# Two projections as seven block products, their weight sums, branch merge and residual carried by accumulating transfers

## The chip, the cores and the metric

The kernel runs on one core of one Trainium2 chip. Its engines are TensorE (PE in the profile; PEld is its loading of weights), VectorE (DVE), ScalarE (ACT), GpSimd (POOL) and SyncE (SP, which here only starts transfers). The metric is the device time of one execution in microseconds (us). The kernel before took 1541.7 us as the median of three runs (1539.01 to 1544.57).

## The reference

One layer of an encoder block on 1024 tokens and a model width of 1024. An attention branch and a gated recurrence branch are computed from one input projection; the change lies behind both, where they are projected, merged and projected again:

```python
y_a = einsum('bsc,cd->bsd', o_a * silu(g_a), w_proj_a)           # 512 -> 1024
o_b = rms_norm(o_fwd + o_bwd, hg_norm_w) * silu(g_b)
y_b = einsum('bsc,cd->bsd', o_b, w_proj_b)                       # 1024 -> 1024
merged = sigmoid(zgate_a) * y_a + sigmoid(zgate_b) * y_b
h_res = h_res + einsum('bsd,de->bse', merged, w_out)             # 1024 -> 1024
```

All is float32 at the kernel's edges. Products are computed at float32r speed: each operand is split into a high part (its rounding to float32r) and a low part (the rest), and one product becomes three matmuls: high x high, high x low, low x high.

## The kernel before

**Tiles.** Everything is in tiles of 128 partitions x 512 float32 (256 KB). A weight tile ("page") is loaded from DRAM into `raw`, ScalarE writes its high part `whi`, and GpSimd or VectorE the low part `wlo = raw - whi`; the two rings hold nine pages (`RING`). A matmul is 128 x 128 weights against 128 x 512; a group of them adds up in one PSUM bank.

**Order.** No scheduler runs on the chip. While the program is built, a planner (`Plan`, `Builder`) keeps an estimated clock for each engine. The main line issues matmuls; `tick` lets waiting tasks (`b.task(engine, inputs, function, priority, room)`) issue as soon as their inputs are, by the estimate, nearly ready. The order that comes out is fixed: each engine then works through its own instructions strictly in that order, and an instruction that waits for a semaphore holds up all behind it on its engine. For SP and GpSimd the same holds of starting transfers. SP's transfers take turns on eight semaphores, and each waits for the one eight before it. In the trace nearly all instructions carry line 56, the recording helper, so they are told apart by tile names.

**The end of the kernel.** After the last recurrence head and the last gate pages of the input projection come three projections, one behind the other, 960 matmuls in all:

- y_a: 8 output pages j x 2 token halves, 4 x 3 matmuls each (192). `evac_ya` multiplies the bank with the sigmoid gate (`sgl`, loaded from the scratch tensor `sgD`) into `ma`.
- y_b: the same 16 groups of 8 x 3 matmuls (384). The operands `sh`, `sl` are split from `ld`, loaded from `obD`, the branch's transposed output. `evac_yb` multiplies with the gate on VectorE, adds `ma` on GpSimd, and splits the sum into `mh` and `ml` (ScalarE, VectorE).
- out: 2 column halves e x 8 token tiles t, 8 x 3 matmuls each (384). `evac_out` adds the input tile `xr` on VectorE and SP stores the result.

The norm weight `hwc` is folded into w_proj_b's pages while they are split (`b.scales`). w_proj_b's low parts come from VectorE for that reason, those of w_proj_a and w_out from GpSimd. PSUM is three banks for groups of matmuls (`b.gps`) and five for the rest (`b.bank`).

Of the kernel before, what the change touches and what calls it, by code (L numbers as in the profile page):

```python
# [113 lines left out]
class Plan:  # L114
# [24 lines left out]
    def note(self, key, op, args, kw):  # L139
# [6 lines left out]
        out, ins = aps[0], aps[1:]  # L146
# [5 lines left out]
        n = _free(out)  # L152
        pace, late = 0.2, 0.1
# [57 lines left out]
class Builder:  # L211
# [361 lines left out]
def hybrid_block(ctx, tc, a, out):  # L573
# [78 lines left out]
    consts.tile([128, 48], F32, name="pad")  # L652
    eps = consts.tile([128, 1], F32, name="eps")
# [39 lines left out]
    xs = {}  # L693
# [135 lines left out]
    pos = 0  # L829
# [1013 lines left out]
    for h in range(8):  # L1843
# [6 lines left out]
        for u in range(2):  # L1850
            b.run_unit([T_group(pos, u, evac_q(h, u), u == 1)])
        pos += 2
    OA, OB = {}, {}
    ectx = {}

    def end_start():
        bctx.close()
        ectx["ep"] = ep = ctx.enter_context(tc.tile_pool(name="end", bufs=1))
        ectx["ld"] = b.ring(ep, "ld", 6, [128, 512])
        for k in range(8):  # L1860
            b.task("sp", [oaD], lambda k=k: split_load(OA, k % 4, k // 4, oaD[k % 4, k // 4],
                                                       lambda n: ep.tile([128, 512], F32R, tag="L", name=n, bufs=17)),
                   4, ectx["ld"].soon)

    def split_load(to, j, half, src, new):
        t = ectx["ld"].get()
        s_.dma_start(t, src)
        b.task("act", [t], lambda: split_store(to, j, half, t, new), 4)

    def split_store(to, j, half, t, new):  # L1870
        hi, lo = new(b.name("sh")), new(b.name("sl"))
        a_.activation(hi, t, AF.Copy)
        v_.tensor_tensor(lo, t, hi.bitcast(F32), op=OP.subtract)
        ectx["ld"].done(t)
        to[j, half] = (hi, lo)

    n = 0
    for j in range(TAIL, 8):
        for half in range(2):
            b.run_unit([T_group(pos, half, evac_sg(1, j, half), half == 1)])  # L1880
# [5 lines left out]
        end_start()  # L1886
        b.drain()
    hctx.close()
    assert pos == b.ops - 40, pos

    ep = ectx["ep"]
    ob = ctx.enter_context(tc.tile_pool(name="endo", bufs=1, side="right"))
    MA, MH, ML = {}, {}, {}
    for half in range(2):
        for h in range(8):
            k = 8 * half + h
            b.task("sp", [obD], lambda h=h, half=half: split_load(  # L1900
                OB, h, half, obD[h, half], lambda n: ob.tile([128, 512], F32R, name=n)), 4, ectx["ld"].soon)
    def sig_load(w, j, half):
        t = ep.tile([128, 512], F32, tag="sg", name=b.name("sgl"), bufs=4)
        s_.dma_start(t, sgD[w, j, half])
        b.task("act", [t], lambda: (a_.activation(t, t, AF.Sigmoid), open_.add((w, j, half))), 1)
        return t

    def three(wp, xs, c):
        (wh, wl), (xh, xl) = wp, xs
        return [(wh[:, c:c + 128], xh), (wh[:, c:c + 128], xl), (wl[:, c:c + 128], xh)]  # L1910

    def evac_ya(j, half, sg):
        def f(ps):
            t = ep.tile([128, 512], F32, tag="Hh", name=b.name("ma"), bufs=18)
            b.until(lambda: (0, j, half) in open_)
            v_.tensor_tensor(t, ps, sg, op=OP.mult)
            b.gps.done(ps)
            MA[j, half] = t
        return f

    def evac_yb(j, half, sg):
        def f(ps):
            b.until(lambda: (1, j, half) in open_)
            v_.tensor_tensor(sg, ps, sg, op=OP.mult)
            b.gps.done(ps)
            ma = MA.pop((j, half))
            g_.tensor_tensor(sg, sg, ma, op=OP.add)
            hi = ep.tile([128, 512], F32R, tag="Hh", name=b.name("mh"), bufs=18)
            lo = ep.tile([128, 512], F32R, tag="L", name=b.name("ml"), bufs=17)
            a_.activation(hi, sg, AF.Copy)  # L1930
            v_.tensor_tensor(lo, sg, hi.bitcast(F32), op=OP.subtract)
            MH[j, half], ML[j, half] = hi, lo
        return f

    sgs, open_ = {}, set()
    seq = [(0, j, half) for j in range(8) for half in range(2)] + [(1, j, half) for j in range(8) for half in range(2)]

    def ahead(k):
        while len(sgs) < min(len(seq), k + 3):
            sgs[seq[len(sgs)]] = sig_load(*seq[len(sgs)])  # L1940

    k = 0
    for w in range(2):
        for j in range(8):
            for half in range(2):
                ahead(k)
                sg = sgs[w, j, half]
                k += 1
                if w == 0:
                    gr = dict(k=4, step=lambda d, half=half: three(b.w[pos], OA[d, half], 128 * d),  # L1950
                              evac=evac_ya(j, half, sg), need=lambda d: pos + 1)
                    if half:
                        gr["free"] = lambda d: pos + (d + 1) // 4
                else:
                    gr = dict(k=8, step=lambda d, half=half: three(b.w[pos + d // 4], OB[d, half], 128 * (d % 4)),
                              evac=evac_yb(j, half, sg), need=lambda d: pos + d // 4 + 1,
                              ready=lambda half=half: all((h, half) in OB for h in range(8)))
                    if half:
                        gr["free"] = lambda d: pos + (d + 1) // 4
                b.run_unit([gr])  # L1960
            pos += 1 if w == 0 else 2

    def evac_out(e, t, x):
        def f(ps):
            o = stage.get()
            v_.tensor_tensor(o, ps, x, op=OP.add)
            b.gps.done(ps)
            s_.dma_start(out[128 * t:128 * t + 128, 512 * e:512 * e + 512], o)
            stage.done(o)
        return f  # L1970

    for e in range(2):
        grs = []
        for t in range(8):
            half, c = divmod(t, 4)
            x = ep.tile([128, 512], F32, tag="sg", name=b.name("xr"), bufs=4)
            s_.dma_start(x, a["x"][t, :, 512 * e:512 * e + 512])

            def step(d, half=half, c=c):
                wh, wl = b.w[pos + d]  # L1980
                s = slice(128 * c, 128 * c + 128)
                return [(MH[d, half][:, s], wh), (MH[d, half][:, s], wl), (ML[d, half][:, s], wh)]

            gr = dict(k=8, step=step, evac=evac_out(e, t, x), need=lambda d: pos + d + 1)
            if t >= 6 and (e == 0 or t == 7):
                gr["free"] = lambda d: pos + d + 1
            if t < 6 or e == 1:
                b.run_unit([gr])
            else:
                grs.append(gr)  # L1990
        if grs:
            b.run_unit(grs)
        pos += 8
    b.drain()


# [101 lines left out]
```

## Time and profile before

| quantity | value |
|---|---|
| median of three runs | 1541.7 us |
| profiled execution, span | 1541.9 us |
| PE busy | 1502.3 us (97%), 8109 matmuls |
| DVE busy | 964.9 us (63%) |
| ACT busy | 806.4 us (52%) |
| POOL busy | 433.2 us (28%) |
| DMA | 186.05 MB, mean 121 GB/s |
| last three projections | from 1320.6 us to the end |

The profile gives for each engine its busy time, for groups of equal instructions their number, mean duration and the idle time ahead of them with what ended it, and for transfers the time from issue to landing. Tile names stand without buffer numbers: `gp` is a PSUM bank of a matmul group. Matmuls are pipelined: the duration that is shown for one overlaps the next, so the distance from start to start is what one costs in a row of them.

### The profile page before, as it was taken

To read this page: it belongs to the slowest core of one execution; us is meant where nothing else is said; L and a number is where in the kernel's file an instruction comes from. 1 tells how busy PE (TensorE), PEld (TensorE's weight loads), DVE (VectorE), ACT (ScalarE), POOL (GpSimd) and SP (SyncE) were. 2 spreads that over 40 slices of the span, in tenths; PEclk is the share of its full clock that TensorE was granted. 3 is DMA by queue.
4 is the path that set the end of the run, shared out by engine and by line. 5 is a ranking of instruction groups with operands and counts; after the bars stand their busy time and mean duration, and the time that the engine had idled before them with its cause. 6 is when DMAs were issued, how large, how long until landed. Compare 5 with 4: busy or idle time off the path is not lost. (4 is left out here: it accounts for less than half of the span.)

```text
span 1541.9 us, 22959 instructions
## 1 busy us (share of the span) xinstructions
PE 1502.3 (97%) x8109; PEld 1232.8 (80%) x8109; DVE 964.9 (63%) x1937; ACT 806.4 (52%) x1665; POOL 433.2 (28%) x424
## 2 busy tenths in 40 slices
PE   8999999999999999999989999999989999999999
PEld 7788888777778787888867788878878878888887
DVE  6791778687887834544333558889888886633211
ACT  5542667566676646776722255556554742733210
POOL 0022333232334230110113452444233432013320
PEclk9999999999999999999989999999999999999999
DMA  5443242442424457564256531131311312933232
GB/s 197 132 164 111 97 142 84 135 120 61 135 69 110 109 163 242 191 214 150 83 150 216 173 117 41 42 100 52 96 28 42 109 49 68 328 107 105 84 119 92
DMA packets 163767, 186.05 MB, mean 121 GB/s; under 512 B 42763, under 2 KB 99107, under 8 KB 163652
## 3 DMA queue, kind: packets, MB, share of 16 engines
q1 hardware_dynamic: 156228, 184.13, 38.2%
q10 hardware_dynamic: 7424, 0.45, 0.3%
q8 instruction: 64, 1.05, 0.3%
q14 instruction: 51, 0.42, 0.1%
HBM read 128.60 MB, written 60.66 MB: 123 GB/s over the span
## 5 line engine op out<-in xcount | busy, mean ns | idle before, releaser
L56 POOL TENSOR_TENSOR wlo<-raw,whi 128x512 fp32r<-128x512 f32 x119 | 160.6, 1356 | 431.6 <-ACT whi L56 412.0
L56 POOL TENSOR_TENSOR wlo<-qraw,whi 128x512 fp32r<-128x512 f32 x100 | 139.8, 1406 | 293.0 <-ACT whi L56 263.6
L56 PE MATMUL gp<-whi,hh 128*128 128x512 f32 x344 | 141.2, 411 | 2.8 <-ACT hh L56 1.4
L56 ACT ACTIVATE whi<-raw 128x512 fp32r<-128x512 f32 x136 | 85.0, 625 | 104.7 <-PE gp L56 79.4
L56 PE MATMUL gp<-hh,whi 128*128 128x512 f32 x336 | 137.8, 410 | 0.0
L56 PE MATMUL gp<-whi,hl 128*128 128x512 f32 x344 | 135.9, 395 | 1.3 <-DVE hl L56 1.3
L56 PE MATMUL gp<-wlo,hh 128*128 128x512 f32 x344 | 135.6, 394 | 0.0
L56 PE MATMUL gp<-hh,wlo 128*128 128x512 f32 x336 | 132.0, 393 | 0.0
L56 PE MATMUL gp<-hl,whi 128*128 128x512 f32 x336 | 131.6, 392 | 0.0
L56 ACT ACTIVATE whi<-qraw 128x512 fp32r<-128x512 f32 x140 | 86.0, 624 | 54.0 <-DVE qraw L56 33.6
L56 DVE CUSTOM_DVE_ANT_0 as<-sc,abias 128x192 f32<-128x192 f32 (+2 forms) x192 | 56.2, 348 | 92.8 <-PE sc L56 57.5
L56 ACT ACTIVATE stage<-gp 128x512 f32<-128x512 f32 x60 | 35.4, 594 | 113.6 <-PE gp L56 92.5
L56 ACT ACTIVATE as<-as,neg 128x192 f32<-128x192 f32 (+2 forms) x192 | 83.5, 438 | 7.9 <-DVE neg L56 7.9
L56 DVE TENSOR_TENSOR qraw<-qraw,qraw 128x512 f32<-128x512 f32 x80 | 67.3, 843 | 30.7 <-POOL wlo L56 23.6
L56 PEld LDWEIGHTS gp<-whi,hh 128*128 128x128 f32 x344 | 65.5, 190 | 24.1 <-issue 5.9
L56 PEld LDWEIGHTS gp<-whi,hl 128*128 128x128 f32 x344 | 65.4, 190 | 16.3 <-DVE hl L56 2.2
L56 PEld LDWEIGHTS gp<-wlo,hh 128*128 128x128 f32 x344 | 65.7, 191 | 12.2 <-issue 0.2
L56 PE MATMUL gp<-sh,whi 128*128 128x512 f32 x192 | 74.7, 389 | 0.0
L56 PE MATMUL gp<-sl,whi 128*128 128x512 f32 x192 | 74.7, 389 | 0.0
L56 PE MATMUL gp<-sh,wlo 128*128 128x512 f32 x192 | 74.7, 389 | 0.0
L56 PEld LDWEIGHTS gp<-hh,wlo 128*128 128x128 f32 x336 | 63.4, 189 | 14.0
L56 PEld LDWEIGHTS gp<-hh,whi 128*128 128x128 f32 x336 | 63.7, 190 | 11.4
(257 smaller groups left out, 3980.3 us busy)
## 6 DMA issues: line engine op xcount, KB each, us to landing
raw<-in_w_in_dram SPq DMA_DIRECT2D x112, 256.0 KB, 2.7
qraw<-in_w_in_dram SPq DMA_DIRECT2D x80, 256.0 KB, 4.3
qkD<-ny SPq DMA_DIRECT2D x48, 256.0 KB, 2.1
igD<-stage SPq DMA_DIRECT2D x32, 256.0 KB, 2.0
ig<-igD SPq DMA_DIRECT2D x32, 256.0 KB, 4.4
sgl<-sgD SPq DMA_DIRECT2D x32, 256.0 KB, 3.6
sgD<-stage SPq DMA_DIRECT2D x26, 256.0 KB, 2.0
ak<-qkD SPq DMA_DIRECT2D x6, 1024.0 KB, 7.9
```

Of the source, the lines that this page charges most:

```text
L56: got = f(*args, **kw)
```

## The change

The first projection (y_a) keeps its 192 matmuls, now with all groups of token half 0 first. Each of the two 1024 x 1024 projections is cut into 2 x 2 blocks of 512 and computed by seven block products in place of eight (Winograd's form of Strassen's scheme). A product is 4 groups u of 12 matmuls: 336 matmuls in place of 384 for each projection. `SEVEN` is their order. With weight blocks W11, W12, W21, W22 (first figure: half of the inner dimension) and data blocks X(token half, inner half):

| product | weights | data |
|---|---|---|
| 11 | W11 | X00 |
| 21 | W21 | X01 |
| T2 | W11 + W12 + W22 | X10 - X00 - X11 |
| T1 | W11 + W12 | X10 - X11 |
| T3 | W12 + W22 | X00 - X10 |
| 22 | W22 | X01 + (the T2 data) |
| T4 | W21 + W11 + W12 + W22 | X11 |

- **Weight sums** are made by transfers that add to what lies at their destination (`more`, issued on GpSimd's queue): T3's page is W12 with W22 added from DRAM, T2's is W11 with T3's page added from SBUF, T4's is W21 with T2's page added, T1's is a second copy of W12 with W11 added from DRAM. That is 16 such transfers for each projection, issued in the order T3 and T2 by turns (i = 0 to 3), T4, T1.
- **Data sums** (16 for each projection) are made on VectorE, in place. All 28 pages and 28 data tiles of each projection are split into high and low parts, all low parts now on VectorE; before it was 16 pages and 16 data tiles.
- **Evacuation.** Products that add to a bank that is used again are copied out by ScalarE (11, T2, T1) and combined on VectorE (21, T3, 22); T4 leaves the result in the bank.
- **Branch merge**: 16 accumulating transfers add the gated y_b to `ma`, in place of 16 additions on GpSimd.
- **Residual**: for three of the four output blocks the input is added by accumulating transfers from DRAM (12), for the fourth on VectorE as before.
- The gate ring `sg` has three buffers; `hwc` is applied when the recurrence output is evacuated; PSUM is reopened as four and four banks ahead of y_a; the planner counts an issue on GpSimd as 1.0 us.

In the built program PE has 96 instructions fewer, VectorE 108 more, ScalarE 72 more; GpSimd loses 32 subtractions and additions and issues 60 transfers; SP has four fewer. Up to the first matmul of y_a the order on every engine is the same in both programs, but for the early loads that the new ending needs.

```diff
-            self.t[key] = start + 0.08
+            self.t[key] = start + (1.0 if key == "pool" else 0.08)
...
-    items += [wpa[i] for i in range(8)] + [wpb[i] for i in range(16)] + [wo[i] for i in range(16)]
+    items += [wpa[i] for i in range(8)]
...
-    for i in range(16):
-        b.scales[b.ops - 32 + i] = hwc
...
-        a_.activation(t, ps, AF.Copy)
+        a_.activation(t, ps, AF.Copy, scale=hwc)
...
+        ectx["acc"] = b.ring(ep, "acc", 8, [128, 512])
+        ectx["xh"] = b.ring(ep, "xh", 8, [128, 512], F32R)
+        ectx["xl"] = b.ring(ep, "xl", 8, [128, 512], F32R)
+        ectx["sg"] = b.ring(ep, "sg", 3, [128, 512])
...
+    psum(4)
...
+    rawq = b.ring(ob, "eraw", 18, [128, 512])
...
+    SEVEN = ("11", "21", "T2", "T1", "T3", "22", "T4")
...
+    def more(dst, src):
+        g_.dma_start(dst, src, accum_op=OP.add)
...
+    def seven_weights(base, pages, along=None):
...
+        for k, ms in enumerate((("11",), ("21",), ("12", "22"), ("1b",))):
+            for i in range(4):
+                for m in ms:
+                    b.task("sp", [], lambda m=m, i=i: load(m, i), 2, lambda: rawq.soon() and b.wire())
+            for f in along[k] if along else ():
+                b.task("sp", [obD], f, 2, b.wire)
...
+        for i in range(4):
+            mix("T3", i, "12", "22")
+            mix("T2", i, "11", "r12", (("11", i), ("mix", "T3", i)))
+        for i in range(4):
+            mix("T4", i, "21", "r11", (("21", i), ("T2", i)))
+        for i in range(4):
+            mix("T1", i, "1b", "11")
...
+    def seven_sides(X):
...
+        for i in range(4):
+            mix("T3", i, (0, 0), (0, 0), (1, 0), OP.subtract, ("11",))
+            mix("T2", i, "s2", (1, 1), (0, 0), OP.subtract)
+        for i in range(4):
+            mix("T1", i, (1, 0), (1, 0), (1, 1), OP.subtract)
+            mix("22", i, (0, 1), (0, 1), "s2", OP.add, ("21",))
...
+    def seven(base, pairs, tok, A, E, kept, fin, ready):
...
+        def evac(op, u):
+            if op == "11":
+                keep(p, op, u, bankA[u])
+            elif op == "21":
+                add("11", u, p[u], bankE[u])
+                E.done(bankE[u])
+                fin(0, 0, u, p[u], None)
+            elif op == "T2":
+                keep(q, op, u, bankA[u])
+            elif op == "T1":
+                keep(r, op, u, bankE[u])
+            elif op == "T3":
+                add("T1", u, r[u], bankA[u], "bank")
+                fin(1, 1, u, r[u], None)
+            elif op == "22":
+                add("T2", u, q[u], bankE[u], "tile")
+                E.done(bankE[u])
+                fin(0, 1, u, q[u], None)
+            else:
+                fin(1, 0, u, bankA[u], A)
+
+        for o, op in enumerate(SEVEN):
+            for u in range(4):
...
+                for k in range(4):
+                    n = base + 4 * o + (k if tok else u)
+                    b.until(lambda: b.split_next > n and (op, k) in pairs)
...
+        def gate():
+            d = t if bank_ is None else sgs[sg]
+            v_.tensor_tensor(d, t, sgs[sg], op=OP.mult)
...
+            b.task("pool", [d], lambda: merge(d), 2)
+
+        def merge(d):
+            ma = MA[j, half]
+            more(ma, d)
...
+    seven(b.ops, pairs_b, False, b.gps, b.bank, lambda *_: None, fin_b, None)
+    pairs_o = seven_sides(M)
...
+    seven(b.ops + 28, pairs_o, True, b.bank, b.gps, fold, fin_o, lambda op, u: (op, u) in folded)
```

With `tok` false (y_b, called B below) group u of a product needs only page u; with `tok` true (out, called O below) every group needs all four pages.

More of the change, by code (lines that the diff above doesn't have):

```diff
@@ L1888, in hybrid_block @@
     hctx.close()
-    assert pos == b.ops - 40, pos
-    ep = ectx["ep"]
+    assert pos == b.ops - 8, pos
+    psum(4)
+    ep, acc, sgr = ectx["ep"], ectx["acc"], ectx["sg"]
     ob = ctx.enter_context(tc.tile_pool(name="endo", bufs=1, side="right"))
[L1896 to L1901, printed above, removed]
+    rawq = b.ring(ob, "eraw", 18, [128, 512])
@@ new lines, in load_ob, with near, in_order, go @@
+    def load_ob(h, half):
+        t = ob.tile([128, 512], F32, name=b.name("ob"))
+        s_.dma_start(t, obD[h, half])
+        X[half, h // 4, h % 4] = t
+    SEVEN = ("11", "21", "T2", "T1", "T3", "22", "T4")
+    SIDES = ("11", "21", "22")
+    def near(tiles):
+        return b.when_all(tiles) and all(b.p.free(t) <= b.p.t["pe"] + b.AHEAD for t in tiles)
+    def more(dst, src):
+        g_.dma_start(dst, src, accum_op=OP.add)
+    def in_order(work):
+        at = [0]
+        def go(f):
+            at[0] += 1
+            f()
+        for k, (op, eng, ready, f) in enumerate(work):
+            b.task(eng, [], lambda f=f: go(f), 2 + 0.1 * SEVEN.index(op), lambda k=k, ready=ready: at[0] == k and ready())
@@ new lines, in seven_weights, with load, split, f @@
+    def seven_weights(base, pages, along=None):
+        raw = {}
+        def load(m, i):
+            raw[m, i] = rawq.get()
+            s_.dma_start(raw[m, i], pages["12" if m == "1b" else m][i])
+        for k, ms in enumerate((("11",), ("21",), ("12", "22"), ("1b",))):
[4 more added lines that the diff above has]
+                b.task("sp", [obD], f, 2, b.wire)
+        work, mixes, n, did = [], [], [base], set()
+        def split(op, m, i, last):
+            k = n[0]
+            n[0] += 1
+            def f():
+                b.split(raw[m, i])
+                did.add((op, i))
+                if last:
+                    rawq.done(raw[m, i])
+            work.append((op, "act", lambda: (m, i) in raw and (op in SIDES or ("mix", op, i) in did) and b.when_all([raw[m, i]])
+                         and b.split_next == k and k < b.freed + b.RING, f))
+        def mix(op, i, dst, src, after=()):
+            def f():
+                more(raw[dst, i], raw[src[1:], i] if src[0] == "r" else pages[src][i])
+                did.add(("mix", op, i))
+                if op == "T4":
+                    rawq.done(raw["11", i])
+            mixes.append((op, "pool", lambda: (dst, i) in raw and all(k in did for k in after) and near([raw[dst, i]]), f))
+        for op in SEVEN:
+            for i in range(4):
+                m = {"T2": "11", "T1": "1b", "T3": "12", "T4": "21"}.get(op, op)
+                split(op, m, i, op not in ("11", "21", "T2"))
+        for i in range(4):
[5 more added lines that the diff above has]
+            mix("T1", i, "1b", "11")
+        in_order(work)
+        in_order(mixes)
@@ L1902, in sig_load @@
     def sig_load(w, j, half):
-        t = ep.tile([128, 512], F32, tag="sg", name=b.name("sgl"), bufs=4)
+        t = sgr.get()
         s_.dma_start(t, sgD[w, j, half])
+        sgs[w, j, half] = t
         b.task("act", [t], lambda: (a_.activation(t, t, AF.Sigmoid), open_.add((w, j, half))), 1)
[L1906 to L1912, printed above, removed]
+    MA, M = {}, {}
@@ L1935, in hybrid_block @@
[L1935 to L1943, printed above, removed]
-        for j in range(8):
[L1945 to L1988, printed above, removed]
-            else:
[L1990 to L1993, printed above, removed]
+    AT = (("21", 0, 0), ("T3", 1, 1), ("22", 0, 1), ("T4", 1, 0))
@@ new lines, in hybrid_block, with x_load, fold, f @@
+    seven(b.ops, pairs_b, False, b.gps, b.bank, lambda *_: None, fin_b, None)
+    pairs_o = seven_sides(M)
+    xr, folded = {}, set()
+    def x_load(op, half, e, u):
+        t = sgr.get()
+        r0 = 4 * half + u
+        s_.dma_start(t, a["x"][r0, :, 512 * e:512 * e + 512])
+        xr[op, u] = t
+    for u in range(4):
+        b.task("sp", [], lambda u=u: x_load("T4", 1, 0, u), 1, sgr.soon)
+    def fold(op, u, t):
+        half, e = {"11": (0, 0), "T1": (1, 1), "T2": (0, 1)}[op]
+        def f():
+            more(t, a["x"][4 * half + u, :, 512 * e:512 * e + 512])
+            folded.add((op, u))
+        if op == "T2":
+            folded.add((op, u))
+        else:
+            b.task("pool", [t], f, 1)
@@ new lines, in fin_o, with out_, late @@
+    def fin_o(half, e, u, t, bank_):
+        r0 = 128 * (4 * half + u)
+        ring, o = acc, t
+        if bank_ is not None:
+            b.until(lambda: ("T4", u) in xr)
+            ring, o = sgr, xr["T4", u]
+            v_.tensor_tensor(o, t, o, op=OP.add)
+            bank_.done(t)
+        def out_():
+            s_.dma_start(out[r0:r0 + 128, 512 * e:512 * e + 512], o)
+            ring.done(o)
+        def late():
+            more(o, a["x"][4 * half + u, :, 512 * e:512 * e + 512])
+            b.task("sp", [o], out_, 1)
+        if (half, e) == (0, 1):
+            b.task("pool", [o], late, 1)
+        else:
+            b.task("sp", [o], out_, 1)
```

149 lines of the change are left out of this document (120 added, 29 removed).

## The prediction

> **What bounds the kernel now.** I read the page's busy shares first, then the chain that ended last, then the ending in stretches.
>
> ```profile
> span 1541.9 us, 22959 instructions
> PE 1502.3 (97%) x8109; PEld 1232.8 (80%) x8109; DVE 964.9 (63%) x1937; ACT 806.4 (52%) x1665; POOL 433.2 (28%) x424
> ```
>
> ```profile
> 1308.45 229.88 PE gp L56 x1014
> 1538.34 0.02 issue
> 1538.36 0.69 DVE stage L56
> ```
>
> ```profile
> core 0: us, PE busy (x) PEld busy (x) DVE busy (x) ACT busy (x) POOL busy (x), PEclk, DMA share, GB/s
> 1320.00:1365.00 45.00, 45.00 (x201) 37.24 (x200) 28.38 (x43) 27.16 (x45) 0.41 (x1) 1.00 0.77 256
> 1365.00:1451.00 86.00, 86.00 (x381) 71.23 (x380) 26.55 (x38) 26.88 (x46) 29.59 (x23) 1.00 0.29 91
> 1451.00:1542.00 91.00, 87.32 (x386) 71.97 (x384) 12.44 (x18) 5.58 (x9) 11.64 (x9) 1.00 0.35 107
> ```
>
> The chain ends in 1014 matmuls without a gap, and the three stretches of the ending show PE full and every other engine well below. TensorE alone sets the ending. What a matmul costs there is read from the groups' first and last starts:
>
> ```profile
> L56 PE MATMUL gp<-sh,whi x192: 389/389/389, 1320.6 to 1450.4; 128*128 128x512 f32 x192
> L56 PE MATMUL gp<-whi,ml x128: 388/389/389, 1451.6 to 1537.9; 128*128 128x512 f32 x128
> ```
>
> 960 matmuls start between 1320.6 and 1537.9: 217.3 / 959 = 0.2266 us each. The 389 ns shown overlap; they are no price.
>
> **What is removed.** 2 x 48 matmuls x 0.2266 = 21.8 us, all of it on the path. The 1.3 us additions on GpSimd, its subtractions, and `hwc` in the weight splits were hidden under PE and give nothing back. Up to y_a nothing else moves, and behind the last matmul stay one VectorE addition and a store. So the question is whether PE can still be fed. One product now takes 48 x 0.2266 = 10.9 us, a group of 12 takes 2.72.
>
> **The unknown: an accumulating transfer.** No row of this trace has one, nor any transfer from GpSimd. The nearest are plain 256 KB transfers, and at the far end one of 1024 KB:
>
> ```profile
> sgl<-sgD SPq DMA_DIRECT2D x32, 256.0 KB, 3.6
> ld<-obD SPq DMA_DIRECT2D x16, 256.0 KB, 5.6
> raw<-in_w_out_dram SPq DMA_DIRECT2D x16, 256.0 KB, 3.1
> out_dram<-stage SPq DMA_DIRECT2D x16, 256.0 KB, 2.0
> raw<-in_w_proj_b_dram SPq DMA_DIRECT2D x13, 256.0 KB, 2.8
> GB/s 204 326 395 386 344 173 57 145 136 72 113 79 127 75 128 64 120 71 128 62 138 66 69 79 90 103 104 101 96 100 210 120 111 106 89 113 79 114 82 59
> ```
>
> ```profile
> ak<-qkD SPq DMA_DIRECT2D x6, 1024.0 KB, 7.9
> ```
>
> ```profile
> 1537.93 0.39 PE L56 MATMUL gp<-whi,ml 128*128 128x512 f32 x1
> 1538.36 0.69 DVE L56 TENSOR_TENSOR stage<-gp,xr 128x512 f32<-128x512 f32 x1 [4.75 <-PE gp L56]
> 1539.08 0.33 SPq L56 DMA_DIRECT2D out_dram<-stage  x1
> ```
>
> Call L the time from issue to landing. Bounds: 2.0 (the fastest 256 KB) and 7.9 (four times the bytes). I take 4.1: a weight page lands in 2.8; adding needs the destination read too, another 256 KB at the best 395 GB/s, 0.7; and an issue takes 1.0 by the planner's edit where SP's takes 0.33, another 0.6 to 0.7. This is nearer the weight page's row than the 1024 KB row.
>
> The page "DMA: Bandwidth & Descriptors" of the Trainium skill (Anatomy of one DMA) fits a transfer issued by GpSimd as 2.0 us plus its bytes at 436 GB/s; from that I estimate 2.6 us, and the sum below would be 1545. It gives no price for adding, and no run here shows one yet. "Collectives: The Full Stack" (The bandwidth ceiling) speaks against this change: adding needs two source reads and halves the rate; with twice the bytes the estimate is 3.2 us, and the sum 1550.
>
> **Where PE waits.** The walk goes by each engine's order in the built program. Prices: ScalarE 0.62, VectorE 0.69 to 0.73 a tile, hand-over 0.02 and the last matmul's 0.16 behind its slot.
>
> ```profile
> L56 ACT ACTIVATE sgl<-sgl 128x512 f32<-128x512 f32 x32 | 19.7, 624 | 17.4 <-DMA sgl<-sgD 17.0
> L56 DVE TENSOR_TENSOR sl<-ld,sh 128x512 fp32r<-128x512 f32 x19 | 13.3, 726 | 1.0 <-ACT sh L56 0.8
> L56 DVE TENSOR_TENSOR sgl<-gp,sgl 128x512 f32<-128x512 f32 x16 | 11.1, 692 | 23.2 <-PE gp L56 23.2
> ```
>
> ```profile
> 1320.81 0.60 ACT L56 ACTIVATE stage<-gp 128x512 f32<-128x512 f32 x1 [1.30 <-issue]
> ```
>
> *1. Start of y_a.* PSUM is reopened, and the first matmul waits for the copy of the last gate group, which runs from 1320.8 to 1321.4, where y_a now starts at 1320.6: 0.9.
>
> *2. T2 of B, page 3 of 0 to 3.* On GpSimd stand T3 and T2 for i = 0, T3 and T2 for i = 1, merge of group 0, T3 and T2 for i = 2, merges of groups 1 to 3, T3 and T2 for i = 3. Each T2 waits until its T3 has landed. From the first matmul of B: last y_a gate, 1.0, which SP's next gate load waits for; behind it SP brings a page, eight data tiles and W12, eleven tiles or 2.9 MB at 395 GB/s, 7.3, the last landing about 2 later, 9.5; T3 and T2 of i = 0, 2L; split and three VectorE tiles up to gate 0, 2.9; merge issue and handing over, 1.3; T3 and T2 of i = 2, 2L; split, low part, gate 3, 2.1; only that gate frees the buffer for SP's load ahead of the last W12 page, whose landing I put at 5.6, as `ld` in its burst; T3 and T2 of i = 3, 2L; split 0.7. Sum 23.1 + 6L. PE wants the page after two products and three groups, 30.0. It waits 6L - 6.9 = 17.7.
>
> *3. T1 of B.* Its first page is issued behind T4's four, of which the last waits for T2's page 3: 1.0 + L less one group, 2.72: 2.4. Not below 1.9, since ScalarE first splits a data tile and copies T2's last bank.
>
> *4. Start of O.* ScalarE has the split of a T2 page of O ahead of O's first data tile, and it waits for the first T3 and T2. Their W12 is loaded behind a gate load, which waits for the gate of product 22's last group: the gate ring has three buffers, and the loads, ScalarE and VectorE now go round it. From the first matmul of T3: split of the first T4 page behind the end of T1 and three VectorE tiles, 5.5; gate load, 4.0; two on ScalarE, 1.3; fourteen VectorE tiles (low parts, additions, gates), 10.1; gate load, 4.0; ScalarE 1.3; three VectorE, 2.2; gate and W12, 5.0; 2L; two splits, 1.3. Sum 34.7 + 2L against three products, 32.7: 2.0 + 2L = 10.2. Loads stand between 3.6 and 5.6 of the rows.
>
> *5. T2 of O, page 3* (all four pages before the first group). From O's late start, T2's first page landed 1.3 before: two issues between, residual folds with them, 3.0; ScalarE, 1.9; a fold, 1.0; split, 0.6; and five landings in a row, 5L; seven accumulating transfers that read 3.7 MB in about 7 us, 9.3 at 395 GB/s, add 2.3. Sum 7.5 + 5L against two products and three pages, 23.8: 5L - 16.3 = 4.2.
>
> *6. T1 of O.* The add of product 21's last group stands on VectorE behind T2's last low part; SP's store waits for it, the loads of T1's pages behind that store. Seven VectorE tiles, 5.0; store issue and load, 3.5; L; seven on ScalarE, 4.4. Sum 12.9 + L against 10.9: 2.0 + L = 6.1.
>
> *7. Low parts* a little behind their high parts at five of these places: 1.5.
>
> Waits: 0.9 + 17.7 + 2.4 + 10.2 + 4.2 + 6.1 + 1.5 = 43.0. Less 21.8: +21.2 on the execution's 1541.9, 1563; the median of the runs, 1541.7, is the same to 0.2.
>
> The bounds by the same formulas: L = 2.0 gives waits of 19.4 (place 3 at its floor, 5 at nothing), 1540; L = 2.8 gives 26.6, 1547; L = 6 gives 71.5, 1592; L = 7.9 gives 100, 1620. Even at L = 0 places 1, 3, 4, 6 and 7 keep 8.3. VectorE's 108 instructions more are some 78 us in some 240: it is not the bound, but it stands in the links above.
>
> **Rivals.** Within 0.3% (4.6 us) a measurement of this kernel can't be told from no change.
> - *A plain transfer's price.* L of 1.75 to 2.75, about as the store and the weight page have it: the waits eat the gain, 1544 at 2.5. The skill's fit, 2.6, falls here. For it: 2.0 and 2.8 stand in the rows. Against it: those are not adding, and not issued by GpSimd.
> - *Slow adding.* L of 5.5 to 7.9, above all if GpSimd's transfers share the engines with SP's bursts (`ld` 5.6): 1607 for L = 7.
> - *Faster.* The chain of six landings at place 2 is short enough that T2's pages come before 30 us: L below 1.75. At 1.5 the waits are 0.9 + 2.1 + 1.9 + 5.0 + 0 + 3.5 + 1.5 = 14.9, 1535. Against it: no 256 KB row lands below 2.0. For it: page sums from SBUF don't touch DRAM.
>
> **How the numbers follow.** Forecast case (L from 2.75 to 5.5: 1546 to 1584) 0.66; plain price 0.11; slow 0.16; faster 0.07. So slower by over 0.3% is 0.82, within 0.11, faster 0.07. Likeliest 1563. For eight in ten the range leaves out the faster case, a part of the plain price and the far end of the slow one: 1544 to 1600 (L = 6.6).
>
> **What would show it.** PE with 8013 matmuls and idle ahead of those whose `whi` comes from an `eraw` page, most of it twice: about 18 us some 30 us into B, about 10 at the start of O, released by ScalarE, and ScalarE there waiting for a transfer. GpSimd's transfers landing some 4 us after issue. The distance of matmuls still 0.2266. Wrong would be: PE full through B (then the order of the queue isn't what binds), a landing far from 4.1 (each us is about 13 us of time), or new gaps in y_a or behind the last matmul.

## The result and the profile after

The changed kernel took 1581.4 us as the median of four runs (1573.65 to 1582.37) against 1541.3 us for the kernel before, a ratio of 1.025 (95% interval 1.022 to 1.028): slower, on the forecast's side and inside its range of 1544 to 1600, but 18 us above the 1563 that was given as likeliest. The profiled execution has a span of 1578.9 us, 37.0 above the one of before.

The page of the changed kernel, its busy shares:

```profile
PE 1497.9 (95%) x8013; PEld 1222.6 (77%) x8013; DVE 1029.4 (65%) x2045; ACT 844.9 (54%) x1737; POOL 444.2 (28%) x452
```

The 96 matmuls are gone, and TensorE's share fell with them: it now waits. The timeline of TensorE in the ending shows where; the bracket is the idle time ahead of a matmul and what ended it:

```profile
1318.77 0.47 PE L56 MATMUL gp<-xh,whi 128*128 128x512 f32 x1 [0.84 <-ACT stage L56]
...
1390.42 0.80 PE L56 MATMUL sA<-xh,whi 128*128 128x512 f32 x1 [3.37 <-ACT whi L56]
1391.02 0.63 PE L56 MATMUL sA<-xl,whi 128*128 128x512 f32 x1
1391.44 0.63 PE L56 MATMUL sA<-xh,wlo 128*128 128x512 f32 x1
...
1397.47 0.50 PE L56 MATMUL sA<-xh,whi 128*128 128x512 f32 x1 [1.55 <-ACT whi L56]
...
1414.95 0.80 PE L56 MATMUL sA<-xh,whi 128*128 128x512 f32 x1 [13.02 <-ACT whi L56]
...
1423.73 0.80 PE L56 MATMUL sE<-xh,whi 128*128 128x512 f32 x1 [3.54 <-ACT whi L56]
...
1477.77 0.80 PE L56 MATMUL sA<-whi,xh 128*128 128x512 f32 x1 [8.90 <-ACT xh L56]
...
1509.94 0.80 PE L56 MATMUL sA<-whi,xh 128*128 128x512 f32 x1 [6.46 <-ACT whi L56]
...
1524.17 0.49 PE L56 MATMUL sE<-whi,xh 128*128 128x512 f32 x1 [2.40 <-ACT whi L56]
...
1574.55 0.39 PE L56 MATMUL sA<-whi,xl 128*128 128x512 f32 x1
```

The waits stand at the predicted places, and the idle time adds up to 41.8 us where 43.0 were predicted. That agreement misleads. Behind most waits the matmuls do not start 0.2266 us apart but 0.427 (the rows at 1391.02 and 1391.44): TensorE runs at about half speed there. The windows of the same trace give the granted clock, which was 1.00 from 1362 to 1378 us (columns: length; busy time of PE, PEld, DVE, ACT and POOL, each with its instructions; granted clock; DMA share; GB/s):

```profile
1378.00:1400.00 22.00, 17.08 (x60) 12.71 (x60) 12.68 (x22) 5.33 (x10) 7.84 (x9) 0.83 0.73 134
1400.00:1428.00 28.00, 11.44 (x30) 8.20 (x29) 7.29 (x11) 8.30 (x15) 8.76 (x10) 0.65 0.92 200
```

So idle time is not what a place costs. What it costs is read from start to start: the distance between the first matmuls of two places, less 0.2266 us for each matmul between them. Slow matmuls count in it.

| place of the prediction | predicted | idle in the trace | cost from start to start |
|---|---|---|---|
| 1 start of y_a | 0.9 | 0.8 | 0.8 |
| 2 T2 of B (324 matmuls from 1318.77 to 1414.95) | 17.7 | 17.9 | 22.8 |
| 3 T1 of B (12 to 1423.73) | 2.4 | 3.5 | 6.1 |
| 4 start of O (192 to 1477.77) | 10.2 | 8.9 | 10.5 |
| 5 T2 of O, page 3 (105 to 1509.94) | 4.2 | 6.5 | 8.4 |
| 6 and 7, T1 of O to the end (230 to 1574.55) | 7.6 | 4.1 | 12.5 |
| sum | 43.0 | 41.8 | 61.1 |

61.1 - 21.8 = 39.3. y_a could have started at 1317.9, 2.7 us earlier than before (1320.6), and behind the last matmul 4.35 us are left in place of 4.0: 39.3 - 2.7 + 0.3 = 36.9, the 37.0 of the spans. (Why y_a begins earlier was not traced.)

There were two readings of the missing 18 us: matmuls at half clock, a term that the prediction did not have, or pages that come later than predicted, with the slow matmuls lying in time that would be waited out anyway. The transfers of the ending (columns: KB each, median us from issue to landing), with the share of the DMA engines by queue (q0 is GpSimd's, q1 SP's; window 1318 to 1578):

```profile
q0 software_dynamic: 8640, 15.73, 37.4%
q1 hardware_dynamic: 15696, 28.58, 33.0%
...
eraw<-in_w_proj_b_dram SPq DMA_DIRECT2D x20, 256.0 KB, 4.8
eraw<-in_w_out_dram SPq DMA_DIRECT2D x20, 256.0 KB, 5.3
...
eraw<-eraw POOLq DMA_DIRECT2D x16, 256.0 KB, 4.3
...
eraw<-in_w_proj_b_dram POOLq DMA_DIRECT2D x8, 256.0 KB, 5.2
eraw<-in_w_out_dram POOLq DMA_DIRECT2D x8, 256.0 KB, 5.8
```

60 accumulating transfers took 37.4% of 16 engines for 260 us: 0.374 x 260 / 60 = 1.62 us of all engines each. The landing depends on what else is under way. The chain of waits has these pieces among others (start, us, what):

```profile
1379.41 3.37 DMA eraw<-eraw
1385.84 3.88 DMA eraw<-eraw
...
1393.48 3.28 DMA eraw<-eraw
...
1406.20 4.18 DMA eraw<-in_w_proj_b_dram
...
1415.85 8.94 DMA eraw<-in_w_proj_b_dram
...
1476.08 7.49 DMA eraw<-in_w_out_dram
...
1511.63 7.40 DMA eraw<-in_w_out_dram
```

These sums from SBUF, none of which was issued behind another transfer that adds and was still under way, landed in 3.3 to 3.9 us. One whose operand comes from DRAM took 4.2 so, 7.5 among merges (1476.08) and 8.9 behind T4's four sums and another one (1415.85). Such transfers queue: T4's first three sums of B, issued 0.54 us apart behind the last T2 sum, landed after 4.3, 5.4 and 6.6 us. The row at 1511.63 is no sum but SP's plain load of a T1 page of O, behind T4's sums: 7.4.

### The profile page after: what moved, and what is told of

The parts are those of the page before. It is cut to its first block, busy times and chain, and to the rows that moved or that the text cites. A ratio compares the mean times of both kernels' runs of the same rounds, so it can differ in the third digit from the quotient of the medians.

```text
span 1578.9 us, 23034 instructions
## 1 busy us (share of the span) xinstructions
PE 1497.9 (95%) x8013; PEld 1222.6 (77%) x8013; DVE 1029.4 (65%) x2045; ACT 844.9 (54%) x1737; POOL 444.2 (28%) x452
## 3 DMA queue, kind: packets, MB, share of 16 engines
q1 hardware_dynamic: 155652, 183.08, 36.9%
q0 software_dynamic: 8640, 15.73, 6.2%
q8 instruction: 63, 1.03, 0.3%
## 5 line engine op out<-in xcount | busy, mean ns | idle before, releaser
L56 POOL TENSOR_TENSOR wlo<-raw,whi 128x512 fp32r<-128x512 f32 x103 | 140.3, 1370 | 383.2 <-ACT whi L56 369.2
L56 ACT ACTIVATE whi<-raw 128x512 fp32r<-128x512 f32 x120 | 75.0, 625 | 69.6 <-PE gp L56 44.6
L56 DVE TENSOR_TENSOR wlo<-eraw,whi 128x512 fp32r<-128x512 f32 x56 | 37.7, 689 | 78.4 <-ACT whi L56 78.4
L56 PEld LDWEIGHTS gp<-hl,whi 128*128 128x128 f32 x336 | 63.4, 189 | 11.0
L56 ACT ACTIVATE whi<-eraw 128x512 fp32r<-128x512 f32 x56 | 33.8, 623 | 69.6 <-DMA eraw<-eraw 43.6
```

The costliest lines, as they stand in the source:

```text
L56: got = f(*args, **kw)
```

## The experiments

The theory at the start was: TensorE waits for pages at the end of chains of landings, and the 18 us more are matmuls at half clock behind the waits. The rivals: the new transfers hold up others on the DMA engines; GpSimd's way of issuing; VectorE's 108 more instructions; a clock that falls for another reason than waiting.

### The kernel before, with idle stretches put in

```diff
                 b.run_unit([gr])
+                if w and half:
+                    hi = OB[0, 0][0]
+                    for _ in range({0: 2, 2: 5, 4: 9, 6: 18}.get(j, 0)):
+                        v_.tensor_scalar(hi, hi.bitcast(F32), 1.0, 0.0, op0=OP.mult, op1=OP.add)
```

> The kernel before with four idle stretches put into the second projection: 2, 5, 9 and 18 VectorE instructions that rewrite the operand the next group of matmuls needs, ahead of which TensorE therefore waits about 2, 4, 7 and 13 us (evacuation 0.69 plus 0.69 each). Nothing else changes, and there is no accumulating transfer. Theory (the matmuls of the changed kernel ran slowly because TensorE's granted clock falls behind an idle stretch): no fall behind the 2 us, perhaps one behind the 4 us, half clock for one or two intervals of about 3.4 us behind the 7 and 13 us, with matmuls 0.427 us apart; each costs 1.7 to 3.4 us beside its gap. Gaps 26, clock 5 to 9: 1573 to 1577. Rival (the clock falls for the load that the new transfers or products put on the chip): full clock behind all four, matmuls 0.2266 us apart, 1568.

It took 1584.7 us (one run; 1541.6 before), above both forecasts, mostly since TensorE stood still for longer than meant. The timeline of TensorE at the four stretches, with two matmuls behind the third:

```profile
1378.87 0.79 PE L56 MATMUL gp<-sh,whi 128*128 128x512 f32 x1 [4.37 <-DVE sh L56]
...
1409.31 0.77 PE L56 MATMUL gp<-sh,whi 128*128 128x512 f32 x1 [5.85 <-DVE sh L56]
...
1442.68 0.77 PE L56 MATMUL gp<-sh,whi 128*128 128x512 f32 x1 [8.63 <-DVE sh L56]
1443.25 0.63 PE L56 MATMUL gp<-sl,whi 128*128 128x512 f32 x1
1443.67 0.63 PE L56 MATMUL gp<-sh,wlo 128*128 128x512 f32 x1
...
1479.09 0.77 PE L56 MATMUL gp<-sh,whi 128*128 128x512 f32 x1 [12.92 <-DVE sh L56]
```

The stretches came out at 31.8 us, not 26; no stretch of 2 us was made, so the shortest that was tried is 4.4. Behind each of the four the granted clock falls (0.72 to 0.76 in windows of 12 to 15 us around them), and the matmuls start 0.43 us apart for a while. From the first matmul of the three projections to the last it is 41.7 us more than 0.2266 each; less the 31.8 of waiting that is 9.9, about 2.5 for each stretch, and the 41.7 are nearly the whole of the 43 us. No accumulating transfer is in this kernel: the clock falls because TensorE has waited. The Trainium skill, "TensorE: Matmul & The Clock Gate" (What's actually happening), has the same: the clock is judged over windows of about 3.4 us, and an idle one halves it. The falls behind these four stretches agree; no run here measures the window. Where nothing else is late, as here, the slow matmuls are paid.

### The changed kernel, its waits filled with matmuls

```diff
+    FILL = {(False, "T2", 1, 0): 14, (False, "T2", 2, 0): 14, (False, "T2", 3, 0): 58, (False, "T1", 0, 0): 20,
+            (True, "11", 0, 0): 36, (True, "T2", 0, 3): 30, (True, "T1", 0, 0): 16, (True, "T1", 0, 1): 6}
...
+                    fill = FILL.get((tok, op, u, k), 0)
+                    for _ in range(fill):
+                        b.nc.tensor.matmul(out, zeros, wh if op == "11" else pairs[op, 0][0], start=(op in ("11", "T1") and k == 0),
                                           stop=False, skip_group_check=True)
```

> The changed kernel with 194 matmuls more, zero weights into the same bank, ahead of the eight groups for which TensorE waited longest: 14, 14 and 58 ahead of the second to fourth group of T2 and 20 ahead of T1 in the first seven products, 36 ahead of product 11, 30 ahead of page 3 of T2, 16 and 6 ahead of pages 0 and 1 of T1 in the second. They need nothing that the groups wait for, so they run inside the waits. Theory (about 18 us of the loss are matmuls at half clock behind idle stretches): the pages come as late as before, but the matmuls behind them are 0.2266 us apart: 1562 to 1567. Rival (the slow matmuls have another cause, and the waits are all that an idle TensorE costs): 1579 or above, matmuls still 0.427 us apart at the same places.

It took 1580.6 us (1579.1 to 1582.2), a ratio of 1.026 (1.024 to 1.029): nothing came back. The windows over T2 and T1 of B, in the changed kernel and in this one:

```profile
1385.00:1432.00 47.00, 25.51 (x77) 18.40 (x76) 19.12 (x31) 15.34 (x28) 14.85 (x17) 0.71 0.83 173
```

```profile
1385.00:1432.00 47.00, 45.10 (x190) 34.85 (x189) 20.25 (x33) 17.51 (x32) 14.55 (x17) 1.00 0.82 173
```

The clock stayed at 1.00 there, as meant, and TensorE still waited for the pages behind the filling:

```profile
1413.02 0.50 PE L56 MATMUL sA<-xh,whi 128*128 128x512 f32 x1 [0.72 <-ACT whi L56]
...
1421.66 0.50 PE L56 MATMUL sE<-xh,whi 128*128 128x512 f32 x1 [0.80 <-ACT whi L56]
```

The pages came hardly earlier. T2's page 3 is used 95.7 us behind the start of y_a (1317.29 here), where the changed kernel has 96.2, and T1's first 104.4 against 105.0. So the theory falls in its second half: in B the matmuls at half clock cost some 0.6 us, since a later landing ends the wait behind them. In O the filling is no clean test. The clock was 0.86 there from 1477 to 1500 us, T2's page 3 was used 4.4 us later than in the changed kernel, and most of that was made up by the end; it shows only that the whole got no shorter. "TensorE: Matmul & The Clock Gate" of the Trainium skill (HAM oscillation) prices a throttled stretch at half its length; a loss of that kind showed in the kernel with the idle stretches and not in B of this one. What was left for the 18 us were later pages.

### The same transfers without adding

```diff
-        g_.dma_start(dst, src, accum_op=OP.add)
+        g_.dma_start(dst, src)
```

> The changed kernel with every accumulating transfer replaced by a plain one from GpSimd's queue in the same place: sums, merge and residual are left out (the destination is overwritten). Theory (what PE waits for is the landing of a transfer that adds, several in a row): landing falls from 4.3 to 5.8 to about 3, the waits by the prediction's formulas to about 29 with the clock's loss at about 10: 1559. Rival 1 (GpSimd's way of issuing is what is late, not the adding): landing and time as in the changed kernel, 1575 to 1582. Rival 2 (a transfer that adds occupies the DMA engines twice as long and holds up SP's loads): landing of SP's loads falls too, from 4.8 and 5.3 towards 3, and the time to 1550.

It took 1553.1 us (1548.0 to 1558.3), ratio 1.008 (1.005 to 1.011): 28 us less than the changed kernel, for nothing but the adding. Its transfers in the same window:

```profile
q1 hardware_dynamic: 15696, 28.58, 33.2%
q0 software_dynamic: 4800, 15.73, 18.0%
...
eraw<-in_w_proj_b_dram SPq DMA_DIRECT2D x20, 256.0 KB, 3.9
eraw<-in_w_out_dram SPq DMA_DIRECT2D x20, 256.0 KB, 4.1
...
eraw<-eraw POOLq DMA_DIRECT2D x16, 256.0 KB, 2.9
...
eraw<-in_w_proj_b_dram POOLq DMA_DIRECT2D x8, 256.0 KB, 3.8
eraw<-in_w_out_dram POOLq DMA_DIRECT2D x8, 256.0 KB, 3.1
```

The same 15.73 MB take 18.0% of the engines in place of 37.4%, 0.78 us a transfer in place of 1.62: adding halves the rate. The Trainium skill, "Collectives: The Full Stack" (The bandwidth ceiling), tells the same of the adding step of a collective. GpSimd's way of issuing is excluded as the cause of these 28 us. The theory's 1559 and the second rival's 1550 both come near, and the rows have something of each: the sums land 1.4 to 2.7 us sooner, and SP's loads, of which nothing was changed, 0.9 and 1.2 sooner. How the 28 us divide between the two stays open. Without any adding the kernel is still 0.8% slower than the one before: chains of plain landings hold TensorE up too, the longest wait, at the last page of T2 of B, being 8.2 us.

### The same transfers, loads allowed earlier

```diff
-    def seven_weights(base, pages, along=None):
+    def seven_weights(base, pages, along=None, lead=1.0):
...
-                    b.task("sp", [], lambda m=m, i=i: load(m, i), 2, lambda: rawq.soon() and b.wire())
+                    b.task("sp", [], lambda m=m, i=i: load(m, i), 2, lambda: rawq.soon() and b.p.wire <= b.p.t["pe"] + lead)
...
-                b.task("sp", [obD], f, 2, b.wire)
+                b.task("sp", [obD], f, 2, lambda: b.p.wire <= b.p.t["pe"] + 5)
...
-    seven_weights(b.ops, wB, (obs[:8], obs[8:], (), ()))
+    seven_weights(b.ops, wB, (obs[:8], obs[8:], (), ()), 5)
...
-    seven_weights(b.ops + 28, wO)
+    seven_weights(b.ops + 28, wO, None, 5)
```

> The changed kernel with one number changed: the planner lets SP issue the loads of weight pages and data tiles of the two projections when its estimate of the DMA wire is up to 5 us ahead of TensorE, not 1 us. The same transfers, the same adding, the same work on VectorE; W12 and W22 are loaded during the first projection, where GpSimd stands idle, and no longer behind gate loads. Theory (the chain of landings begins too late, so that PE meets its end): T2's pages of the first seven products come before they are needed, 21 us of waits go there and most of the clock's loss, some 10 us of waits stay in the second: 1531 to 1537, faster than the kernel before. Rival 1 (the price of adding itself, whatever the order): the waits stay, 1570 to 1582. Rival 2 (VectorE's 108 instructions more hold up the splits): no change, 1579.

It took 1552.8 us (1550.3 to 1556.7), ratio 1.009 (1.006 to 1.011). T2 of B has no wait left, and ahead of T1 there is one of 3.7 us that ends with a data tile, not with a page. So SP's order had held place 2, not the landing alone; and VectorE's work is the same, so it was not VectorE. But the forecast missed by 16 us: waits of 5.4, 1.5, 4.6 and 3.3 us stand in O, from its start to T1. The transfers of this kernel (window 1318 to 1546), and the window of products T2 and T1 of B (columns as above):

```profile
eraw<-in_w_out_dram SPq DMA_DIRECT2D x20, 256.0 KB, 6.1
...
eraw<-in_w_proj_b_dram POOLq DMA_DIRECT2D x8, 256.0 KB, 7.8
eraw<-in_w_out_dram POOLq DMA_DIRECT2D x8, 256.0 KB, 7.2
```

```profile
1385.00:1410.00 25.00, 20.49 (x78) 15.63 (x77) 12.77 (x20) 10.19 (x19) 9.17 (x11) 0.86 1.04 224
```

With the loads moved together the landings of page loads and sums lengthen, the sums from DRAM to over 7 us, and in that window the DMA engines are full (share 1.04). The transfers that add are no work in the background: what is moved closer together on the DMA engines waits there.

### Weight sums on GpSimd, or merges on GpSimd

```diff
-        for k, ms in enumerate((("11",), ("21",), ("12", "22"), ("1b",))):
+        for k, ms in enumerate((("11",), ("21",), ("12", "22"))):
...
-                more(raw[dst, i], raw[src[1:], i] if src[0] == "r" else pages[src][i])
+                other = raw[src[-2:], i]
+                g_.tensor_tensor(raw[dst, i], raw[dst, i], other, op=OP.subtract if op == "T1" else OP.add)
...
-            mix("T1", i, "1b", "11")
+            mix("T1", i, "11", "22", (("mix", "T4", i),))
```

> The changed kernel with the 32 weight sums computed by GpSimd in SBUF (additions and subtractions of two tiles, about 1.3 us each, as the 1.3 us additions of the kernel before) in place of accumulating transfers. T1's page is then T2's sum less W22, so the second copy of W12 is not loaded. Merge and residual stay accumulating transfers (28), and VectorE's and ScalarE's work stays what it is. Theory (T2's, T1's and O's first pages are late because each is one or two landings of an accumulating transfer, which take 4 to 8 us and occupy the DMA engines twice as long as a plain one): a sum is ready 1.4 us after its page, place 2, 5 and 6 all but vanish, some 10 us of waits stay at T1 of the first seven products (behind T4's sums) and at the start of the second: 1530 to 1542. Rival (the seven products' own order, VectorE's 108 instructions more, the splits): the waits stay, 1565 to 1582.

```diff
-            more(ma, d)
+            g_.tensor_tensor(ma, ma, d, op=OP.add)
```

> The changed kernel with only the 16 merges moved back to additions on GpSimd, 1.3 us each; weight sums and residual stay accumulating transfers (44). Theory: four merges no longer stand between the sums of place 2 as issues with transfers of 1.6 us of all DMA engines each, and O's first data tiles are there 1.4 us and not 5.2 to 5.6 us after the gate; place 2 falls by about 8 and the start of O by about 4, the rest stays: 1560 to 1570. Rival (merges lie beside the chain): 1575 to 1582.

The first took 1560.8 us (ratio 1.013, 1.010 to 1.015), the second 1561.1 (1.013, 1.011 to 1.016). Each takes some 20 us off the changed kernel, so both kinds of transfer are on the path; for the merges this is what was expected. For the sums it is some 20 to 30 us more than forecast. There the two longest waits in T2 of B (7.90 and 2.62 us) are ended by VectorE's low parts, and the window around them shows why, of the changed kernel first and then of this one (columns as above):

```profile
1378.00:1408.00 30.00, 19.01 (x64) 13.71 (x63) 15.12 (x25) 8.36 (x15) 8.71 (x10) 0.80 0.77 161
```

```profile
1378.00:1408.00 30.00, 18.15 (x64) 13.20 (x63) 30.00 (x22) 7.61 (x14) 21.32 (x18) 0.83 0.33 71
```

VectorE (the third of the busy times) has 15.12 us of work in the changed kernel, which clears it there, and is full here with fewer instructions, 22 in place of 25: each got longer.

### Sums and merges on GpSimd, loads earlier

The edits of the last three kernels together.

> Weight sums and merges computed on GpSimd, and the loads of pages and data tiles let go when the wire's estimate is up to 5 us ahead of TensorE in place of 1 us; of the 60 accumulating transfers 12 stay, the residual's. VectorE and ScalarE do what they do in the changed kernel. Theory: nothing that TensorE waits for hangs on an accumulating transfer any more, the waits are about 0.9 at the start of the first projection and 1 to 4 at the start of the second, and the 21.8 us of the 96 matmuls come through: 1521 to 1528, faster than the kernel before. Rival (VectorE's 108 more instructions, or two products' pages split where one was, bound the ending): waits of 10 to 40 us stay, 1530 to 1560.

It took 1538.9 us (1535.7 to 1540.3), ratio 0.998 (0.997 to 0.999), 11 us above the upper end of the forecast. In B the longest wait of TensorE is 1.03 us, but 10 us (7.67 and 2.33) stand at the start of O. The windows, and the low parts and sums of the ending (groups: busy us, mean ns), the last two rows from the changed kernel and the kernel before:

```profile
1362.00:1385.00 23.00, 22.54 (x100) 18.34 (x99) 23.00 (x19) 12.73 (x24) 19.93 (x12) 1.00 0.18 60
1385.00:1410.00 25.00, 23.97 (x105) 19.32 (x104) 25.00 (x33) 12.91 (x25) 10.75 (x6) 1.00 0.31 94
```

```profile
L56 DVE TENSOR_TENSOR wlo<-eraw,whi 128x512 fp32r<-128x512 f32 x56 | 53.7, 970 | 7.4 <-ACT whi L56 7.4
L56 POOL TENSOR_TENSOR eraw<-eraw,eraw 128x512 f32<-128x512 f32 x32 | 51.9, 1667 | 47.3 <-DMA eraw<-in_w_proj_b_dram 41.6 <-DMA eraw<-in_w_out_dram 2.1 <-issue 1.9
```

```profile
L56 DVE TENSOR_TENSOR wlo<-eraw,whi 128x512 fp32r<-128x512 f32 x56 | 37.7, 689 | 78.4 <-ACT whi L56 78.4
```

```profile
L56 POOL TENSOR_TENSOR sgl<-sgl,ma 128x512 f32<-128x512 f32 x16 | 20.5, 1284 | 90.4 <-DVE sgl L56 90.4
```

VectorE's low part takes 970 ns where the changed kernel's group has 689 (and where moving the loads alone left it at 689), and GpSimd's sum 1667 where the merge of the kernel before took 1284: they lengthen each other. The Trainium skill has this in "SBUF — State Buffer" (Who interferes with whom): a VectorE instruction with two inputs in SBUF contends with a GpSimd instruction that reads SBUF.

### The same, VectorE relieved

```diff
+            if self.low == "copy":
+                self.p.act.activation(lo, raw, AF.Copy)
...
-    b.low = "dve"
+    b.low = "copy"
```

> The version with all sums and merges on GpSimd and loads up to 5 us ahead, with one thing left out: the low parts of the 56 weight pages of the two seven-product projections are copies made by ScalarE (0.62 us each), not VectorE's subtraction, so VectorE loses 56 instructions of 0.97 us mean, 54 us; the products with the low parts of the weights are not the right ones. TensorE's, GpSimd's and the transfers' work is the same. Theory (VectorE, stretched by GpSimd's additions, is what bounds that version): the 10 us wait at the start of the second projection and the half-clock matmuls behind it shrink to 2 to 6 us in all: 1523 to 1530. Rival (gate loads on SP, or the landing of data tiles, bound it): 1535 to 1540, unchanged.

It took 1527.4 us (1525.4 to 1529.9), ratio 0.993 (0.991 to 0.995). That is 11.5 us less, of which some 3 are not the edit's: the kernel before took 1542.7 us beside the version above and 1539.6 beside this one. So VectorE's work was what held the version above; that it did so only because it was stretched is not shown by this run.

### Each sum where it is cheap

T3's and T2's sums, which are needed at once, and the merges on GpSimd; T4's and T1's sums and the residual by transfers that add; loads up to 5 us ahead; a gate buffer more.

```diff
+                if op in ("T2", "T3"):
+                    g_.tensor_tensor(raw[dst, i], raw[dst, i], raw[src[-2:], i], op=OP.add)
+                else:
                     more(raw[dst, i], raw[src[1:], i] if src[0] == "r" else pages[src][i])
...
-            more(ma, d)
+            g_.tensor_tensor(ma, ma, d, op=OP.add)
...
-        ectx["sg"] = b.ring(ep, "sg", 3, [128, 512])
+        ectx["sg"] = b.ring(ep, "sg", 4, [128, 512])
...
-    rawq = b.ring(ob, "eraw", 18, [128, 512])
+    rawq = b.ring(ob, "eraw", 17, [128, 512])
```

> Sums that are needed at once on GpSimd, sums with time to spare on transfers: of the weight sums T3's and T2's (16) and the 16 merges are computed on GpSimd, T4's and T1's (16) and the residual (12) stay accumulating transfers, loads may again run 5 us ahead, and the gate ring has four buffers (the page ring 17). Against the version with all sums and merges on GpSimd it takes 16 of its 48 additions away. Theory (there GpSimd's additions stretch VectorE's instructions from 0.69 to about 0.97 to 1.07 us, and VectorE, full between 1362 and 1410 us, is what TensorE waits for; transfers cost nothing where the page has a product's time to land): VectorE gets room, the wait at the start of the second seven products falls from 10 to about 6 to 8, 1528 to 1534. Rival (transfers that add hold up SP's loads wherever they stand): T4's and T1's transfers bring the waits back, 1540 to 1555.

It took 1528.9 us (1525.5 to 1531.7), ratio 0.993 (0.992 to 0.995): faster than both kernels, and within 2 us of the one that left VectorE's low parts out. VectorE's low part takes 817 ns in it. The waits that remain in it stand at the start of O:

```profile
1440.07 0.50 PE L56 MATMUL sA<-whi,xh 128*128 128x512 f32 x1 [2.96 <-ACT xh L56]
...
1443.79 0.80 PE L56 MATMUL sA<-whi,xl 128*128 128x512 f32 x1 [2.98 <-DVE xl L56]
```

So transfers that add are not too dear as such: 28 of the 60 are still there, and no wait of TensorE over 0.3 us stands at T1 or T4. The gate buffer more was not tried alone. The prediction put part of the wait at the start of O on the ring of three gate buffers, so what it and the sums that moved each took off that wait is not known.

## Why the prediction was right, and where it was short

*What is removed.* 8013 matmuls, and 21.8 us of TensorE's time: in the last version, with 6 us of waits at the start of O and 0.84 at the start of y_a (10.3 in all from start to start), 11 of them show.

*That PE can't be fed, and where.* Right at every place, released as named: ScalarE's split of an `eraw` page in T2 and T1 of both projections, ScalarE's copy at the start of y_a (0.84 against 0.9), ScalarE's first data tile at the start of O. Place 2 came as three waits (3.37, 1.55, 13.02) and not as one ahead of page 3, with the last the longest. Moving the loads alone removed it.

*The price L.* This is the step that failed, as a size. Taken was 4.1 for every accumulating transfer, and for SP's loads what they showed before. A sum from SBUF took less where none was ahead of it, 3.3 to 3.9, but had a median of 4.3. A sum from DRAM had one of 5.2 and 5.8, SP's weight loads 4.8 and 5.3 where the rows of before had 2.8 and 3.1; without adding these loads had 3.9 and 4.1, so the adding made about half of that. The prediction charged an accumulating transfer for its second operand once, in its own landing, and for queueing in one place only (2.3 at place 5). In the run each held all DMA engines for 1.62 us, and what stood behind it waited, the plain loads too:

- Place 2, 5.1 over: GpSimd issued the first T3 sum 2.0 us later than reckoned, the third T3 sum took 6.6 us to its T2 sum and not 4.1, and from the loads that the last gate let go (1399.18) to the sum on the last W12 page (1406.20) it was 7.0 where 5.6 was put.
- Place 3, 3.7 over: T1's first page was issued at 1415.31, behind T4's sums, and split at 1423.05, 7.7 us later.
- Place 5, 4.2 over: the T3 sum issued at 1476.08 took 7.49.
- Places 6 and 7, 4.9 over: SP's load of a T1 page took 7.40, where store, issue and load were 3.5 together.
- Place 4 was met, 10.5 against 10.2.

That a landing stretches when many are under way stood in the prediction as the cause of the rival of slow adding. The time came out near the upper end of the forecast case (1584, L = 5.5), short of that rival. "Each us of landing is about 13 us of time" is low by the prediction's own formulas: above L = 3.3 they give 15, from 1563 at 4.1 to 1592 at 6. The runs don't test it. Taking the adding out shortened the sums' landings by 1.4 to 2.7 us and the time by 28, but SP's loads came sooner as well.

*"The distance of matmuls still 0.2266"* was wrong. It is 0.427 behind the waits. Its price was next to nothing in B, as the filled waits showed; for O it was not measured by itself. That the idle time came out at 41.8 against 43.0 was luck: part of the longer waiting was filled by slow matmuls and didn't count as idle.

*VectorE is not the bound.* Right for the changed kernel (15.1 busy of 30 us in T2 of B), and with VectorE's work unchanged the moved loads took 28 us off; wrong as soon as GpSimd computes beside it.

## What to carry to other kernels

A transfer that adds in place of an instruction was cheap here only where its result had a product's time to land: price it as two transfers on the DMA engines, for itself and for every load behind it, and keep it out of chains of two or three. Count what a wait costs from start to start, not as idle time, and before a slow clock is blamed fill the wait and see whether the next page comes any earlier. Moving a sum from the DMA to GpSimd moves the cost to VectorE: share the sums out by how soon each is needed.

## What the runs showed of the hardware that was not expected

- An accumulating transfer of 256 KB holds the 16 DMA engines for 1.62 us, the same transfer without adding for 0.78. With none ahead of it a page sum on the chain of waits landed in 3.3 to 4.2 us, behind others in up to 8.9.
- Behind idle stretches of 4.4 to 12.9 us TensorE's matmuls start 0.427 us apart in place of 0.2266, at a cost of about 2.5 us a stretch where nothing else is late. Where a later landing ended the next wait (T2 and T1 of B) it was some 0.6 us for all of them.
- VectorE's subtraction of two SBUF tiles goes from 689 to 970 ns beside GpSimd's additions, which go from 1.28 to 1.67 us.
